# Attention scores and state-space products over 64 rows or over 128 rows with half of them zero

## The chip, the core and the metric

The kernel runs on one core of a Trainium2 chip. Five engines work beside each other, each through its own instructions in order: TensorE (PE, matrix products; PEld is its loading of the stationary operand), VectorE (DVE), ScalarE (ACT), GpSimd (POOL) and SyncE (SP, which issues the DMAs here). They meet through semaphores. The metric is the device time of one execution, in microseconds.

## The reference

One inference step of a two-layer decoder trunk. 512 prompt positions and 8 sample positions pass through the same weights. A layer is a half-step gated feed-forward block, a token mixer and a second feed-forward block, each followed by a layer norm. The mixer projects the input once and splits the columns among three branches and three gates:

```python
def _mixer(x, prev, n_prev_valid, lb, p):
    h = x @ p['w_in'] + p['b_in']
    q, k, v, mz, mxbc, mdt, hq, hf, hi, hg, gates = _split_cols(h)
    ya, nk, nv = _swa_attention(q, k, v, k_prev, v_prev, n_prev_valid, p['att_sinks'])
    ym, nconv, nssm = _mamba2(mz, mxbc, mdt, conv_prev, ssm_prev, ...)
    oh, nhg = _hgrn2(hq, hf, hi, lb, hg_prev)
    ...
    merged = g_att * (ya @ p['w_br_att']) + g_ssm * (ym @ p['w_br_ssm']) + g_hg * (yh @ p['w_br_hg'])
    return merged @ p['w_out'], ...
```

Two products matter here. In the attention there are 8 query heads of width 64 and 2 key heads (groups of 4 query heads share one), with a window of 128 positions:

```python
s = jnp.einsum('bnqkgd,bnskd->bnkgqs', qb, kb) * (HEAD_DIM ** -0.5)     # per key head k, over d = 64
```

In the state-space branch there are 2 groups with a state of width 64, and in each chunk of 128 positions

```python
w = jnp.einsum('bctgn,bcsgn->bctsg', Cc, Bc)[..., None] * decay * dt    # per group g, over n = 64
```

Both sum over 64 elements only, once for each of two groups.

## The kernel before

**Layout.** Activations lie transposed: channels on the 128 partitions, positions along the free dimension (520 columns, the first 512 the prompt's). A projection's 128 output channels are one tile. So one key tile `k` holds key head 0 on rows 0 to 63 and key head 1 on rows 64 to 127, and a query tile `q` of pair i holds head i on the upper rows and head 4+i on the lower. In the state-space branch the tiles `bm` (B) and `cm` (C) hold group 0 on rows 0 to 63 and group 1 on rows 64 to 127.

**The dense products.** Every weight multiplication (`gemm`, lines 166 to 179) splits both operands into a high and a low part and issues three matmuls of 128x128 by 260 columns for each 128 channels, lines 177, 178 and 179 (and 409 to 411 in the feed-forward blocks). Weights come in by DMA (tile `ws`), ACT casts the high part (`wh`, lines 73 and 90) and DVE subtracts it for the low part (`wl`, lines 74 and 91). The small products of the branches are plain f32 matmuls; the trace shows each of these as two MATMUL records, so "x2" below is one of them.

**The mixer.** `mixer` (line 557) emits first the HGRN2 branch (four heads, `hgrn_head`), woven with the input projections; then the four attention pairs, woven with the first merge (gates and output projection of the HGRN2 branch); then the state-space branch (`mamba`), and the two other merges. A scheduler then puts each engine's instructions in order from estimated times and priorities, so that in the built program the small products of a branch stand singly among the dense matmuls.

**Attention.** `attention_pair` (line 1102) takes, for each of four blocks of 128 queries, the scores of both groups: `q[rows]` is stationary, `k[rows]` moves, 128 or 256 columns wide, with `rows` the 64 rows of the group (line 1130). Each lands in a PSUM tile of the tag `s` (three of them). DVE adds the position bias and takes the maximum (line 1136); ACT takes the exponential (1148); DVE divides (1155); PE transposes (1165), the transposes are copied out (1167), and PE multiplies by the values (1175). A layer has 4 pairs x 4 blocks x 2 groups = 32 score matmuls.

**State-space branch.** `mamba` walks over four chunks c. Per chunk, line 939 takes the products of B and C for the two groups, again over 64 rows each; DVE masks them (942), builds the decay (945) and multiplies (947); PE multiplies by the values (954) and the state (960) and forms the new state (968). A layer has 8 matmuls of line 939. The sample positions are updated on DVE and POOL meanwhile (`mamba_sample`).

**Two tiles for the HGRN2 heads.** `self.att` (line 1342) is two tiles of 128x512, set to zero once by POOL at the start. `hgrn_head` writes the allowed places of its decayed products into them (lines 683 to 693, heads 0 and 2 into the first, 1 and 3 into the second) and PE reads them at line 735. The places never written stay zero.

Of the kernel before, what the change touches and what calls it, by code (L numbers as in the profile page):

```python
# [19 lines left out]
P = 128  # L20
NL = 2
NT = 520
TA = 260
TP = 512
# [101 lines left out]
class Kernel:  # L126
# [755 lines left out]
    def mamba(self, l):  # L882
        nc = self.nc
# [11 lines left out]
        bm, cm = xa[4], xa[5]  # L895
# [5 lines left out]
            nc.vector.tensor_copy(self.sp["z"][:, 8 * j : 8 * j + 8], z[j][:, TP:])  # L901

        self.mamba_sample(l, dt, dta)
        y = [self.slot(name="my", cols=TP) for _ in range(4)]
        state = None
        for c in range(4):
            cs = slice(c * P, (c + 1) * P)
            ab = []
            for g in (0, 1):
                a = self.slot(name="mab")  # L910
# [18 lines left out]
            if c:  # L929
                cw_t = self.slot(name="mcw")  # L930
                cw = cw_t[:, :TP].rearrange("p (h t) -> p h t", t=P)
                for g in (0, 1):
                    rows = slice(64 * g, 64 * g + 64)
                    nc.scalar.activation(cw[rows], ab[g][rows], AF.Exp)
                nc.vector.tensor_tensor(cw, cw, cm[:, cs].unsqueeze(1).to_broadcast([P, 4, P]), op=ALU.mult)
            pcb = [self.bank("s"), self.bank("s")]
            for g in (0, 1):
                rows = slice(64 * g, 64 * g + 64)
                nc.tensor.matmul(pcb[g][:, :P], lhsT=bm[rows, cs], rhs=cm[rows, cs], start=True, stop=True)
            for g in (0, 1):  # L940
                cbm = self.sm(P, "cbm")
                nc.vector.tensor_tensor(cbm, pcb[g][:, :P], self.tri, op=ALU.mult)
                for hh in range(4):
                    k = c * 8 + 4 * g + hh
# [4 lines left out]
                for jj in (0, 1):  # L949
                    for e in (0, 1):  # L950
                        hh, rows = 2 * jj + e, slice(64 * g, 64 * g + 64)
# [3 lines left out]
                for jj in (0, 1):  # L955
                    for e in (0, 1):
                        hh, rows = 2 * jj + e, slice(64 * g, 64 * g + 64)
# [9 lines left out]
            for g in (0, 1):  # L967
                nc.tensor.matmul(
                    pst[64 * g : 64 * g + 64, :256], lhsT=btok[:, 64 * g : 64 * g + 64], rhs=xw[:, 256 * g : 256 * g + 256],
                    start=True, stop=True,  # L970
# [7 lines left out]
                nc.vector.tensor_tensor(new, new, pst[:, :256], op=ALU.add)  # L978
            state = new
        nc.sync.dma_start(self.ap["o_pssm"][l], state)  # L980

        ssq = self.slot(name="mss", cols=TP)
        for j in range(4):
# [97 lines left out]
    def attention_lin(self, l, aq):  # L1081
# [13 lines left out]
        for i in range(4):  # L1095
# [3 lines left out]
            aq[i] = q  # L1099
            yield  # L1100

    def attention_pair(self, l, i, aq):
        nc = self.nc
        q, k = aq[i], aq["k"]
        if i == 0:
            vt, v = self.slot(name="avt"), aq["v"]
            p = self.bank("s")
            for n in range(4):
                ns = slice(n * P, (n + 1) * P)
                nc.tensor.transpose(p[:, ns], v[:, ns], self.ident)  # L1110
            nc.scalar.copy(vt[:, :TP], p)
            aq["vt"] = vt
        vt = aq["vt"]
        bias = self.slot(name="abias", cols=TP)
        nc.sync.dma_start(bias, self.ap["c_abias"][:, i * TP : (i + 1) * TP])
        sink = self.par[l][:, 161 + 8 * i : 169 + 8 * i]
        sc = [self.sample_slot() if i % 2 else self.slot(name="asc", cols=TP) for _ in range(4)]
        m, ng, den, es = (self.sm(8, x) for x in ("am", "ang", "aden", "aes"))

        def part(n, g):  # L1120
            w = 2 * P if n else P
            return sc[n][:, 2 * P * g : 2 * P * g + w], w

        yield
        for n in range(4):
            pp = [self.bank("s"), self.bank("s")]
            for g in (0, 1):
                s, w = part(n, g)
                rows = slice(64 * g, 64 * g + 64)
                nc.tensor.matmul(  # L1130
                    pp[g][:, :w], lhsT=q[rows, n * P : (n + 1) * P], rhs=k[rows, (n + 1) * P - w : (n + 1) * P], start=True, stop=True
                )
            for g in (0, 1):
                s, w = part(n, g)
                c = slice(2 * n + g, 2 * n + g + 1)
                nc.vector.tensor_tensor_reduce(
                    out=s, in0=pp[g][:, :w], in1=bias[:, 2 * P * (g + 1) - w : 2 * P * (g + 1)], scale=1.0, scalar=sink[:, c],
                    op0=ALU.add, op1=ALU.max, accum_out=m[:, c],
                )
        yield  # L1140
        nc.vector.tensor_scalar(ng, m, -1.0, None, op0=ALU.mult)
        nc.vector.tensor_tensor(es, sink, m, op=ALU.subtract)
        nc.scalar.activation(es, es, AF.Exp)
        for n in range(4):
            for g in (0, 1):
                s, w = part(n, g)
                c = slice(2 * n + g, 2 * n + g + 1)
                nc.scalar.activation(s, s, AF.Exp, bias=ng[:, c], accum_out=den[:, c])
        nc.vector.tensor_tensor(den, den, es, op=ALU.add)
        nc.vector.reciprocal(den, den)  # L1150
        for n in range(4):
            for g in (0, 1):
                s, w = part(n, g)
                c = slice(2 * n + g, 2 * n + g + 1)
                nc.vector.tensor_scalar(s, s, den[:, c], None, op0=ALU.mult)
        yield

        pt = {}
        for b in (0, 1):
            for g in (0, 1):  # L1160
                p = self.bank("s")
                lo = b * P
                for n in range(b, 4):
                    s, w = part(n, g)
                    nc.tensor.transpose(p[:, n * P : (n + 1) * P], s[:, w - P * (b + 1) : w - P * b], self.ident)
                pt[b, g] = self.slot(name="apt", cols=TP)
                (nc.scalar.copy if g else nc.vector.tensor_copy)(pt[b, g][:, lo:], p[:, lo:])
        yield
        pv = self.bank("s")
        for b in (0, 1):  # L1170
            for n in range(b, 4):
                ns = slice(n * P, (n + 1) * P)
                for g in (0, 1):
                    kb = (n - b) * P + 64 * g
                    nc.tensor.matmul(
                        pv[64 * g : 64 * g + 64, ns], lhsT=vt[:, kb : kb + 64], rhs=pt[b, g][:, ns],
                        start=b == 0 and n == 0, stop=b == 1 and n == 3,
                    )
        yh, yl = self.out_slot(F32R, "yah"), self.out_slot(F32R, "yal")
        nc.scalar.copy(yh[:, :TP], pv)  # L1180
        nc.vector.tensor_tensor(yl[:, :TP], pv, yh[:, :TP].bitcast(F32), op=ALU.subtract)
        self.at_out.append((yh, yl))
        yield
# [360 lines left out]
```

## Time and profile before

| what | value |
|---|---|
| median of 3 runs | 2606.45 us (2605.48 to 2608.71) |
| the profiled execution | 2604.06 us |
| its span, first to last instruction | 2602.3 us |
| busy: PE / DVE / ACT / POOL | 98% / 75% / 48% / 27% |
| mean granted TensorE clock | 0.992 |
| DMA queues' share of the 16 engines' time | 36.3% |

Busy time of PE overlaps itself, because a matmul's record runs on while the next one has started: the cadence is read from the distance between starts. The position in the span tells the stage: the first layer's attention lies at about 556 to 636 us, its state-space chunks at about 723 to 790 us; the second layer's lie about 1290 us later.

### The profile page before, as it was taken

What the parts mean: (1) busy time and instruction counts of PE and PEld (TensorE: products, weight loads), DVE (VectorE), ACT (ScalarE), POOL (GpSimd) and SP (SyncE); (2) the same over time, 40 slices, a digit from 0 to 9 for tenths busy, and PEclk for the clock granted to TensorE, in tenths of its full rate; (3) what the DMA queues carried; (4) which work ended last, traced back from release to release, by engine and by line L of the source; (5) the groups of instructions that cost most, each with busy time, mean ns of one, the idle gap of its engine ahead of it and who ended that gap; (6) DMA issues with size and microseconds to landing.
All of it is one profiled execution on the core that took longest, in us unless ns stands there. A gap on an engine that the chain in (4) does not pass through costs nothing.

```text
span 2602.3 us, 51878 instructions
## 1 busy us (share of the span) xinstructions
PE 2543.6 (98%) x20784; PEld 2474.7 (95%) x20784; DVE 1949.4 (75%) x3690; ACT 1250.4 (48%) x2358; POOL 694.6 (27%) x635
## 2 busy tenths in 40 slices
PE   8999999999999999999999999999999999999997
PEld 8999999898989999999989999999989899999997
DVE  8795988864685598868897858989546845978586
ACT  6352566443534473434663524764435344635255
POOL 1121243300143441212331212433001434413124
PEclk9999999999999999999999999999999999999999
DMA  6332356412242343232532414564123423333233
GB/s 208 105 122 82 127 178 217 149 68 83 99 141 91 122 138 106 90 114 82 186 128 93 141 55 150 171 219 145 57 84 112 139 90 122 138 98 107 89 125 119
DMA packets 134066, 318.17 MB, mean 122 GB/s; under 512 B 20452, under 2 KB 56516, under 8 KB 133824
## 3 DMA queue, kind: packets, MB, share of 16 engines
q1 hardware_dynamic: 133824, 314.86, 36.3%
q8 instruction: 163, 2.67, 0.4%
q14 instruction: 79, 0.65, 0.1%
HBM read 302.93 MB, written 11.88 MB: 121 GB/s over the span
## 4 chain that ended last, share of the span: by engine, by line
PE 73%; DVE 15%; DMA 4%; issue 3%; ACT 3%; POOL 3%; SPq 0%; POOLq 0%; ACTq 0%; DVEq 0%
PE g L177 15%; PE g L178 15%; PE g L179 15%; PE g L409 5%; PE g L411 5%; PE g L410 5%; DVE wl L91 3%; PE s L409 2%; PE s L411 2%; PE s L410 2%; DMA ws<-in_w_gu 1%; PE s L1130 1%; DVE y L249 1%; DMA smp<-r8d 1%; DVE xl L253 1%
## 5 line engine op out<-in xcount | busy, mean ns | idle before, releaser
L177 PE MATMUL g<-xh,wh 128*128 128x260 f32 (+1 forms) x2336 | 669.1, 287 | 7.5 <-ACT xh L1407 5.7
L178 PE MATMUL g<-xl,wh 128*128 128x260 f32 (+1 forms) x2336 | 668.7, 286 | 3.6 <-DVE xl L253 2.7
L179 PE MATMUL g<-xh,wl 128*128 128x260 f32 (+1 forms) x2336 | 668.2, 286 | 1.9 <-DVE wl L91 1.9
L90 ACT CAST wh<-ws 128x1024 fp32r<-128x1024 f32 (+1 forms) x382 | 389.9, 1024 | 376.6 <-PE g L178 252.4
L91 DVE TENSOR_TENSOR wl<-ws,wh 128x1024 fp32r<-128x1024 f32 (+1 forms) x382 | 469.4, 1231 | 117.4 <-ACT wh L90 116.6
L177 PEld LDWEIGHTS g<-xh,wh 128*128 128x128 f32 (+1 forms) x2336 | 439.5, 188 | 17.5 <-issue 6.1
L178 PEld LDWEIGHTS g<-xl,wh 128*128 128x128 f32 (+1 forms) x2336 | 439.2, 188 | 12.0 <-issue 4.2
L179 PEld LDWEIGHTS g<-xh,wl 128*128 128x128 f32 (+1 forms) x2336 | 439.6, 188 | 9.5 <-issue 4.1
L73 ACT CAST wh<-ws 128x1024 fp32r<-128x1024 f32 (+1 forms) x288 | 265.4, 942 | 295.9 <-PE g L178 161.7
L179 PE MATMUL g<-hh,wl 128*128 128x260 f32 x1408 | 396.1, 283 | 0.0
L178 PE MATMUL g<-hl,wh 128*128 128x260 f32 x1408 | 396.0, 283 | 0.0
L177 PE MATMUL g<-hh,wh 128*128 128x260 f32 x1408 | 391.8, 282 | 1.6 <-DVE y L275 1.6
L74 DVE TENSOR_TENSOR wl<-ws,wh 128x1024 fp32r<-128x1024 f32 (+1 forms) x288 | 320.3, 1118 | 87.1 <-ACT wh L73 86.0
L105 POOL TENSOR_TENSOR ws<-ws 128x512 f32<-128x512 f32 x72 | 136.2, 1892 | 632.0 <-DMA ws<-in_w_gu 260.0
L177 PEld LDWEIGHTS g<-hh,wh 128*128 128x128 f32 x1408 | 263.0, 188 | 2.1 <-DVE y L275 2.0
L178 PEld LDWEIGHTS g<-hl,wh 128*128 128x128 f32 x1408 | 264.7, 188 | 0.1
L179 PEld LDWEIGHTS g<-hh,wl 128*128 128x128 f32 x1408 | 264.6, 188 | 0.2
L409 PE MATMUL g<-xh,wh 128*128 128x260 f32 x864 | 246.3, 286 | 2.6 <-ACT wh L73 2.5
L410 PE MATMUL g<-xl,wh 128*128 128x260 f32 x864 | 245.0, 284 | 0.0
L411 PE MATMUL g<-xh,wl 128*128 128x260 f32 x864 | 242.4, 284 | 1.9 <-DVE wl L74 1.9
L409 PEld LDWEIGHTS g<-xh,wh 128*128 128x128 f32 x864 | 164.4, 190 | 4.8 <-ACT wh L73 3.7
L409 PE MATMUL g<-sx,wh 128*128 128x260 f32 x576 | 164.7, 286 | 4.3 <-ACT wh L73 4.3
(407 smaller groups left out, 5721.6 us busy)
## 6 DMA issues: line engine op xcount, KB each, us to landing
ws<-in_w_gu SPq DMA_DIRECT2D x208, 512.0 KB
ws<-in_w_in SPq DMA_DIRECT2D x132, 512.0 KB
ws<-in_w_dn SPq DMA_DIRECT2D x96, 512.0 KB
ws<-in_w_out SPq DMA_DIRECT2D x32, 512.0 KB
ws<-in_w_dn SPq DMA_DIRECT2D x32, 384.0 KB
smp<-r8d SPq DMA_DIRECT2D x48, 256.0 KB
ws<-in_w_br SPq DMA_DIRECT2D x24, 512.0 KB
smp<-in_hgr SPq DMA_DIRECT2D x16, 256.0 KB
```

The source lines that it names most:

```text
L73: nc.scalar.copy(h[:, :n], s[:, :n])
L74: nc.vector.tensor_tensor(lo[:, :n], s[:, :n], h[:, :n].bitcast(F32), op=ALU.subtract)
L90: nc.scalar.copy(h[:, :n], s[:, :n])
L91: nc.vector.tensor_tensor(lo[:, :n], s[:, :n], h[:, :n].bitcast(F32), op=ALU.subtract)
L105: nc.gpsimd.tensor_tensor(pa[:, b], u[:, a], u[:, b], op=ALU.add)
L177: nc.tensor.matmul(out, lhsT=h[:, wc], rhs=xh[:, c0:c1], start=st, stop=False)
L178: nc.tensor.matmul(out, lhsT=h[:, wc], rhs=xl[:, c0:c1], start=False, stop=False)
L179: nc.tensor.matmul(out, lhsT=lo[:, wc], rhs=xh[:, c0:c1], start=False, stop=en)
L249: nc.vector.scalar_tensor_tensor(y, y, gn, rb, op0=ALU.mult, op1=ALU.mult)
L409: nc.tensor.matmul(out, lhsT=h[:, wc], rhs=xh, start=first and k == 0, stop=False, **go)
L410: nc.tensor.matmul(out, lhsT=h[:, wc], rhs=xl, start=False, stop=False, **go)
L411: nc.tensor.matmul(out, lhsT=lo[:, wc], rhs=xh, start=False, stop=k == HK - 1, **go)
```

## The change

The products no longer pick 64 rows of both operands. The stationary operand is the whole tile of 128 rows, with both groups, and the moving operand is a tile in which the other group's 64 rows are zero. The result is the same sum. The two zero-padded tiles are made in the storage of the two `att` tiles: `by_group` zeroes the other group's half on POOL and copies the group's own half on ACT, once per layer for the keys (in the first attention pair) and once per layer for `cm`. In the first layer `restore_heads` sets both tiles back to zero after the state-space branch, because the HGRN2 heads of the second layer rely on it.

```diff
         self.mamba_sample(l, dt, dta)
+        self.by_group(cm)
...
             for g in (0, 1):
-                rows = slice(64 * g, 64 * g + 64)
-                nc.tensor.matmul(pcb[g][:, :P], lhsT=bm[rows, cs], rhs=cm[rows, cs], start=True, stop=True)
+                nc.tensor.matmul(pcb[g][:, :P], lhsT=bm[:, cs], rhs=self.grp[g][:, cs], start=True, stop=True)
...
         nc.sync.dma_start(self.ap["o_pssm"][l], state)
+        if l < NL - 1:
+            self.restore_heads()
...
+    def by_group(self, t):
+        nc = self.nc
+        self.grp = [a.rearrange("p c t -> p (c t)") for a in self.att]
+        for g in (0, 1):
+            rows, other = slice(64 * g, 64 * g + 64), slice(64 - 64 * g, 128 - 64 * g)
+            nc.gpsimd.memset(self.grp[g][other], 0.0)
+            nc.scalar.copy(self.grp[g][rows], t[rows, :TP])
+
+    def restore_heads(self):
+        for t in self.att:
+            self.nc.gpsimd.memset(t, 0.0)
...
             aq["vt"] = vt
+            self.by_group(k)
...
-                rows = slice(64 * g, 64 * g + 64)
                 nc.tensor.matmul(
-                    pp[g][:, :w], lhsT=q[rows, n * P : (n + 1) * P], rhs=k[rows, (n + 1) * P - w : (n + 1) * P], start=True, stop=True
+                    pp[g][:, :w], lhsT=q[:, n * P : (n + 1) * P], rhs=self.grp[g][:, (n + 1) * P - w : (n + 1) * P], start=True, stop=True
                 )
```

Line numbers behind the change are larger: the scores of line 1130 stand at 1146, the new memsets at 1111 and 1116, the new copies at 1112.

On PE the order of all matmuls stays as it was, in both layers; only the operands of the 80 products change. Here is a piece of the difference in the first attention pair of the first layer (`att_1042` is the first of the two tiles, `att_1044` the second, `aq` a query tile, `ak` the keys, `g` and `s` PSUM tiles):

```order
-L1130 MATMUL s<-ak,aq 128x256
-L179 MATMUL g<-xh,wl 128x260
-L1130 MATMUL s<-ak,aq 128x256
-L177 MATMUL g<-xh,wh 128x260
-L178 MATMUL g<-xl,wh 128x260
-L1130 MATMUL s<-ak,aq 128x128
+L1146 MATMUL s<-att_1042,aq 128x256
+L179 MATMUL g<-xh,wl 128x260
+L1146 MATMUL s<-att_1044,aq 128x256
+L177 MATMUL g<-xh,wh 128x260
+L178 MATMUL g<-xl,wh 128x260
+L1146 MATMUL s<-att_1042,aq 128x128
```

Nothing moved: each score keeps its neighbours and reads a zero-padded tile in place of half of the keys.

On POOL four memsets enter per layer, between the last sample products of the HGRN2 branch (lines 780 and 786) and the first convolution tile of the state-space branch (line 811). Before:

```order
L780 TENSOR_TENSOR smp<-smp 128x512
L786 TENSOR_TENSOR smp<-smp 128x512
L811 MEMSET cb 128x3
L814 COPY cb<-scv 128x8x3
L825 COPY pcv<-cb 128x3
```

and after:

```order
L780 TENSOR_TENSOR smp<-smp 128x512
L786 TENSOR_TENSOR smp<-smp 128x512
L1111 MEMSET att_1042 64x512
L1111 MEMSET att_1044 64x512
L1111 MEMSET att_1042 64x512
L1111 MEMSET att_1044 64x512
L811 MEMSET cb 128x3
L814 COPY cb<-scv 128x8x3
```

The first two belong to the keys and the other two to `cm`; the latter pair has to wait until the last scores of the layer have been read.

On ACT the copies of the keys stand far ahead of the first score, among the last two HGRN2 heads (`ho`, `yhh`, `hit` are tiles of these):

```order
 L683 COPY att_1044<-s 64x4x64
+L1112 COPY att_1042<-ak 64x512
 L743 ACTIVATE ho,hss<-s 128x128 x4
 L718 COPY hit<-s 128x512
@@ -394,68 +395,69 @@
 L517 ACTIVATE aq<-g,qb_1054 128x260
 L535 CAST yhh<-hy 128x512
+L1112 COPY att_1044<-ak 64x512
 L543 CAST yhh<-s_o 128x8
```

Each is placed behind the last work that the HGRN2 heads have for its tile on this engine. The two copies of `cm` stand together among the projections of the gate z, and the two memsets of `restore_heads` on POOL about the last chunk. DVE and SP keep their order.

## Rows read from the trace of the kernel before

**Rows 1.** The page, chain that ended last, by engine.
```profile
PE 73%; DVE 15%; DMA 4%; issue 3%; ACT 3%; POOL 3%; SPq 0%; POOLq 0%; ACTq 0%; DVEq 0%
```
**Rows 2.** Stretches: start:end, length, busy us by engine, clock, DMA share, GB/s.
```profile
556.00:600.00 44.00, 44.00 (x338) 38.08 (x338) 24.92 (x77) 20.57 (x53) 0.00 (x0) 1.00 0.22 73
...
723.00:760.00 37.00, 33.64 (x282) 30.18 (x280) 33.52 (x88) 12.12 (x23) 18.01 (x15) 1.00 0.53 169
760.00:790.00 30.00, 29.82 (x257) 26.30 (x258) 27.71 (x77) 11.68 (x21) 11.14 (x11) 1.00 0.28 98
...
2012.00:2049.00 37.00, 34.99 (x269) 30.95 (x269) 33.39 (x87) 11.07 (x21) 17.79 (x15) 0.91 0.56 170
```
**Rows 3.** One line's instructions: count, ns min/median/max, first and last start, forms.
```profile
L1130 PE MATMUL s<-ak,aq x128: 272/376/481, 557.1 to 1916.9; 64*128 64x256 f32 x96, 64*128 64x128 f32 x32
...
L939 PE MATMUL s<-mxa x32: 272/323/374, 723.7 to 2070.2; 64*128 64x128 f32 x32
```
**Rows 4.** Timeline of PE, attention: start, duration, line, operands.
```profile
572.32 0.49 PE L1130 MATMUL s<-ak,aq 64*128 64x128 f32 x2
572.74 0.39 PE L177 MATMUL g<-xh,wh 128*128 128x260 f32 x1
...
576.51 0.28 PE L179 MATMUL g<-xh,wl 128*128 128x260 f32 x1
576.63 0.28 PE L177 MATMUL g<-xh,wh 128*128 128x260 f32 x1
576.84 0.70 PE L1130 MATMUL s<-ak,aq 64*128 64x256 f32 x2
577.47 0.39 PE L178 MATMUL g<-xl,wh 128*128 128x260 f32 x1
577.69 0.28 PE L179 MATMUL g<-xh,wl 128*128 128x260 f32 x1
```
**Rows 5.** Timeline of PE, three scores in a row.
```profile
563.06 1.13 PE L1130 MATMUL s<-ak,aq 64*128 64x256 f32 x6
564.12 0.39 PE L177 MATMUL g<-yhh,wh 128*128 128x260 f32 x1
```
**Rows 6.** Timeline of PE, an f32 product over 128 rows, 260 columns.
```profile
1277.59 0.28 PE L178 MATMUL g<-hl,wh 128*128 128x260 f32 x1
1277.71 0.60 PE L229 MATMUL s<-ht,inv_d 128*128 128x260 f32 x2
1277.95 0.47 PE L179 MATMUL g<-hh,wl 128*128 128x260 f32 x1
1278.27 0.28 PE L177 MATMUL g<-hh,wh 128*128 128x260 f32 x1
```
**Rows 7.** Timeline of PE, an f32 product over 128 rows, 128 columns.
```profile
501.77 0.28 PE L179 MATMUL g<-xh,wl 128*128 128x260 f32 x1
501.89 0.38 PE L738 MATMUL s<-hst,hep 128*128 128x128 f32 x2
502.03 0.37 PE L177 MATMUL g<-xh,wh 128*128 128x260 f32 x1
502.24 0.28 PE L178 MATMUL g<-xl,wh 128*128 128x260 f32 x1
```
**Rows 8.** Timelines, a division on DVE and the transposes behind it.
```profile
578.25 1.40 DVE L1155 TENSOR_SCALAR asc<-asc,aden 128x256 f32<-128x256 f32 x5
...
584.24 1.03 PE L1165 MATMUL s<-ident,asc 128*128 128x128 f32 x8
```
**Rows 9.** POOL's memset of 128x512 as one line's instructions.
```profile
L1332 POOL MEMSET att<- x2: 524/524/524, 1.8 to 2.3; 128x512 f32 x2
```
**Rows 10.** Timelines of POOL, ACT and PE; in brackets idle time before, and releaser.
```profile
641.70 0.10 POOL L811 MEMSET cb<- 128x3 f32 x1 [124.65 <-PE s L1175]
...
557.19 0.58 ACT L1111 COPY avt<-s 128x512 f32<-128x512 f32 x1 [1.48 <-PE s L1110]
...
542.11 1.06 PE L735 MATMUL s<-hit,att 128*128 128x128 f32 x8
```

## The prediction

> **What bounds the kernel now.** I read the page first. In the chain that ended last, PE has 73% and DVE 15% [rows 1], so an edit pays where PE is on that chain and nothing else is late. Then the two stages that the change touches, by stretches. In the attention of the first layer PE is busy for all of 44.00 us, DVE for 24.92 and ACT for 20.57, POOL not at all [rows 2]: PE alone sets the pace there. In the state-space chunks it is otherwise: DVE has 33.52 of 37 us in 723 to 760 and 27.71 of 30 in 760 to 790 [rows 2]; PE waits in the first and both are nearly full in the second. Next the two lines themselves: 128 records of line 1130 and 32 of line 939 [rows 3], two records a product, so 64 scores (48 of 256 columns, 16 of 128) and 16 products of B and C (128 columns). Last the timeline of PE around single products, because PE's busy time overlaps itself: what a product costs is read from starts.
>
> **What one product over 64 rows costs.** Dense matmuls start 0.12 us apart (576.51 to 576.63) [rows 4]. A score of 256 columns starts 0.21 after its predecessor, the next dense matmul 0.63 after the score, the one behind that another 0.22 later [rows 4]. That is 1.06 us from predecessor to second successor, where 0.24 would do without it: 0.82 us. The 0.21 and the 0.22 are each 0.1 above cadence, so PE seems to empty itself before and behind it, and inside it the second record does not overlap the first as it might. With 128 columns the middle step is 0.42 (572.32 to 572.74) [rows 4], and with the same ends 0.85, less 0.24: 0.61 us.
>
> **What one over 128 rows costs.** The trace has f32 products over all rows, standing singly among the same dense matmuls. With 260 columns (line 229): 0.12, 0.24 and 0.32, together 0.68, less 0.24: 0.44 us [rows 6]. With 128 columns (line 738): 0.12, 0.14 and 0.21, together 0.47, less 0.24: 0.23 us [rows 7]. Twice the second is 0.46, so 256 columns cost 0.44 to 0.46; I take 0.44, the row of almost the same width. A single product thus saves 0.82 - 0.44 = 0.38 us at 256 columns and 0.61 - 0.23 = 0.38 at 128: the saving is the two ends and the pause inside, not the columns.
>
> **Scores.** In each layer's attention three scores of 256 columns stand in a row, and three take 1.06 us [rows 5] where one alone takes 0.63: the third adds 0.43 and the second nothing, so two of different groups run beside each other. With the ends (0.21 + 0.22 - 0.24) the three cost 1.25 us; as 128-row products 3 x 0.44 = 1.32. The change loses 0.07 there, twice. The other 58 scores stand singly (42 of 256 columns, 16 of 128; I counted them in the timelines of both layers), and the order on PE stays as it is. 58 x 0.38 = 22.0, less 0.1: 21.9 us. PE has no idle time in that stage into which this could vanish [rows 2].
>
> The Trainium skill speaks against the change at this place. In "TensorE: Matmul & The Clock Gate", Part 3 (packing small matmuls), products in different row groups run concurrently; and in its section "Why this matters for your kernels" a single product over 32 rows takes the time of one over 128. The trace agrees on the first where two such products are neighbours [rows 5]; on the second it differs, since a single one over 64 rows holds the dense stream 0.82 us against 0.44 [rows 4, 6]. By these two rules alone single products would gain nothing, and the sum would be 0.
>
> **What is late next in the attention.** The softmax of one pair runs while PE does the scores of the next. The divisions of pair 0 end on DVE at 578.25 + 1.40 = 579.65, and PE begins to transpose them at 584.24 [rows 8]: 4.6 us to spare. Between these PE does seven single scores of pair 1 (from 572.32 on) and comes 7 x 0.38 = 2.7 us earlier: 1.9 remain. So I charge nothing. DVE and ACT have 19 and 23 us free in 44 [rows 2] and keep up with a stretch that becomes some 6 us shorter.
>
> **Products of B and C.** Each of the 16 stands singly and saves 0.38 on PE, 6.1 us in all. What of it reaches the end lies between 0 and 6.1. Chunks 0 and 1 (four products a layer) lie in the stretch paced by DVE and by the loads that it waits for: nothing. Chunks 2 and 3 lie in 760 to 790, PE on the chain with DVE at 92% [rows 2]: I take half of 8 x 0.38, 1.5 us.
>
> **Memsets and copies.** Eight memsets of 64x512 and two of 128x512 on POOL, eight copies of 64x512 on ACT. A memset of 128x512 took 0.524 us, a copy of 512 columns 0.58 [rows 9, 10]; the half-height forms are not in the trace, so I bound them by 0 and by these. With the cover gone: 10 x 0.52 + 8 x 0.58 = 9.9 us; I take 0, because of the cover. Keys: POOL idles for 124.65 us up to 641.70 [rows 10], and the last read of the second tile by head 3 ends at 542.11 + 1.06 = 543.2 [rows 10], so memset and copy are through by about 545; the first score comes at 557.1 [rows 3]. The memsets for `cm` wait in POOL's queue for the last score; behind them stands line 811, which before the change began at 641.70 after PE's line 1175, later than the scores. The copies for `cm` fall on ACT, 48% busy over the span, among the projections of z, some 14 us before line 939. `restore_heads` holds POOL for 1.05 us in chunk 3 of one layer, where it has 11.14 of 30 us busy [rows 2].
>
> **Sum.** 21.9 + 1.5 = 23.4 us less. Against the profiled execution (2604.06, of which 2602.3 is span) that is 2580.7. This execution lies 2.4 us under the median of the runs shown; from the median, 2606.45 - 23.4 = 2583.0, and that is the forecast.
>
> **Clock.** In 2012 to 2049 the granted clock is 0.91 [rows 2]: 0.09 x 37 = 3.3 us lost, part of the stretch at 1.2 GHz after PE had waited for DVE. The same stage of the first layer has 1.00 [rows 2]. Such a stretch can come or go with shifted waits: 3.3 us either way.
>
> **Rivals.**
> 1. The gain comes back in the softmax. For it: DVE and ACT have in-order queues, and the 1.9 us above is small. Against: 43% of DVE's time is idle in that stage [rows 2]. If pair 1 and pair 3 gave all theirs back, half of 21.9 would be lost: 2606.45 - 11 - 1.5 = 2594.
> 2. A product over 64 rows costs what one over 128 rows costs in the same place, and the longer starts in rows 4 belong to f32 scores as such. Then nothing is gained: 2606. Against it: lines 229 and 738 are f32 too and have the short ends [rows 6, 7]. The second rule of the Trainium skill cited above would give this.
> 3. Slower. PE is held at the first product of each stage, because its padded tile is not ready: the first score (557.1) or line 939 (723.7) waits for POOL's memset or ACT's copy, and behind it on PE stand all dense matmuls. It decides from 11.7 us of waiting a layer (23.4 / 2); at 15 us the time is 2606.45 - 23.4 + 30 = 2613. For it: POOL's queue is in order. Against: the keys' tile would have to be ready 12 + 12 us later than worked out above.
>
> **How the numbers follow.** Forecast 0.83, rival 1 0.12, rival 2 0.03, rival 3 0.02. A measurement of this kernel tells about 0.2% (5 us) from no change. Forecast and rival 1 are faster: 0.95; rival 2 is the same: 0.03; rival 3 slower: 0.02. The range: downward, all of the 6.1 us of line 939 and 3.3 of clock, 2606.45 - 21.9 - 6.1 - 3.3 = 2575; upward it takes in rival 1 with 2594, to 2595 with the runs' own spread.
>
> **What the changed profile would show.** Right: a 256-column product of line 1146 has starts of 0.12, 0.24 and 0.32 around it and one of 128 columns 0.12, 0.14 and 0.21; the first layer's attention (first score to last transpose) is 11 us shorter, as is the second's; stretches 723 to 760 are no shorter; POOL's memsets end long before the first score. Wrong: starts of 0.2 before and behind the padded products (rival 2); idle time of PE before line 1165, released by DVE line 1155 (rival 1); idle time before the first line 1146, released by POOL or ACT (rival 3). A gain above 31 us or below 11 would refute the sum itself.

## The result, and the profile after

The changed kernel takes 2578.56 us (median of 4 runs, 2577.37 to 2583.22) beside 2606.34 for the kernel before: a ratio of 0.9895, interval 0.9878 to 0.9912, so 27.8 us or 1.05% less. Measured again beside other runs of the kernel before (experiment 4) the ratio was 0.9909 (0.9895 to 0.9922). The forecast was 2583.0, the range 2575 to 2595. The profiled execution has a span of 2576.1 us where the one before had 2602.3.

The page's chain by engine and its busy times, which answer to [rows 1]:

```profile
PE 2513.6 (98%) x20784; PEld 2471.3 (96%) x20784; DVE 1948.8 (76%) x3690; ACT 1255.2 (49%) x2366; POOL 694.1 (27%) x645
...
PE 73%; DVE 15%; DMA 4%; issue 3%; POOL 3%; ACT 2%; SPq 0%; POOLq 0%; ACTq 0%; DVEq 0%
```

The number of matmul records is what it was (20784), and the chain has the same shares but for one per cent of ACT. Nothing became the bound that was not. A change that shortens a stage which PE alone paces leaves no mark in the shares; it shows in the stretches. The view of stretches (start:end, length, busy us of PE, PEld, DVE, ACT and POOL, granted clock, DMA share, GB/s), at the places that answer to [rows 2]:

```profile
553.80:597.80 44.00, 44.00 (x379) 42.97 (x378) 27.25 (x85) 21.05 (x54) 0.00 (x0) 1.00 0.23 75
708.00:745.00 37.00, 33.34 (x267) 30.18 (x266) 33.43 (x87) 10.68 (x21) 17.24 (x15) 0.91 0.54 167
745.00:775.00 30.00, 30.00 (x274) 27.58 (x273) 28.32 (x77) 13.00 (x23) 12.50 (x13) 1.00 0.31 100
```

In the first 44 us of the attention PE now does 379 matmul records instead of 338, and its weight loads are busy for 42.97 us instead of 38.08: the dense stream is closed up. In 745 to 775 (before, 760 to 790) 274 records instead of 257 fit into the same 30 us. Only 708 to 745 has not gained, and there the clock is 0.91, which it was not before.

The scores as one line's instructions (count, ns minimum, median and maximum, first and last start), which answer to [rows 3]:

```profile
L1146 PE MATMUL s<-att,aq x128: 270/378/383, 554.9 to 1890.4; 128*128 128x256 f32 x96, 128*128 128x128 f32 x32
```

The median record is as long as before (378 ns against 376), only the longest fell from 481 to 383 ns: durations show little of the gain, starts show all of it. The timeline of PE around single scores, for [rows 4], in the first layer of the changed kernel (start, duration, line, operands):

```profile
567.69 0.28 PE L179 MATMUL g<-yhh,wl 128*128 128x260 f32 x1
567.82 0.38 PE L1146 MATMUL s<-att,aq 128*128 128x128 f32 x2
567.95 0.36 PE L177 MATMUL g<-xh,wh 128*128 128x260 f32 x1
568.16 0.28 PE L178 MATMUL g<-xl,wh 128*128 128x260 f32 x1
...
571.05 0.28 PE L177 MATMUL g<-xh,wh 128*128 128x260 f32 x1
571.17 0.59 PE L1146 MATMUL s<-att,aq 128*128 128x256 f32 x2
571.41 0.47 PE L178 MATMUL g<-xl,wh 128*128 128x260 f32 x1
571.72 0.28 PE L179 MATMUL g<-xh,wl 128*128 128x260 f32 x1
```

Read the starts. A score of 256 columns: 0.12, 0.24, 0.31, together 0.67 where two dense starts alone would be 0.24: it costs 0.43. One of 128 columns: 0.13, 0.13, 0.21, so 0.23. These are the steps of [rows 6, 7]: against [rows 4] the step in front fell from 0.21 to 0.12 and the one from the score to the next dense product from 0.63 to 0.24, while the last rose from 0.22 to 0.31.

How long the whole stages are now is read from two lines, the first transposes of the values and the first product of the attention's sample positions behind the four pairs. Before:

```profile
L1110 PE MATMUL s<-ident,av x8: 272/272/273, 556.6 to 1848.5; 128*128 128x128 f32 x8
...
L1219 PE MATMUL x<-skt,qm x32: 272/274/325, 643.6 to 1936.8; 128*64 128x130 f32 x32
```

and after:

```profile
L1126 PE MATMUL s<-ident,av x8: 272/272/273, 554.4 to 1832.8; 128*128 128x128 f32 x8
...
L1235 PE MATMUL x<-skt,qm x32: 272/274/325, 630.4 to 1910.1; 128*64 128x130 f32 x32
```

First starts give the first layer: 643.6 - 556.6 = 87.0 before, 630.4 - 554.4 = 76.0 after. Taken from the records themselves to the hundredth, the same distance was 87.03 and 86.99 us in the two layers before, 75.93 and 75.96 after. That is 11.10 + 11.03 = 22.1 us, where the scores were forecast at 21.9.

The second stage is that of the state-space chunks, from the first transpose of a chunk (line 918, or 919 where a line stands above it) to the first product of the norm behind them (line 552). All profiled executions side by side, attention in its two layers, then the chunks in theirs:

| kernel | attention | chunks, first layer | chunks, second layer |
|---|---|---|---|
| before | 87.03, 86.99 | 73.76 | 74.96 |
| before, profiled again (b1) | 87.03, 86.99 | 73.75 | 75.01 |
| changed | 75.93, 75.96 | 73.82 | 72.97 |
| changed, again (a4) | 75.93, 75.96 | 72.92 | 73.00 |
| scores alone (a1) | 75.93, 75.96 | 75.09 | 75.09 |
| products of B and C alone (a2) | 87.03, 86.99 | 74.75 | 73.10 |
| no padding (a3) | 75.97, 75.97 | 72.86 | 73.26 |

The attention repeats to 0.05 us from execution to execution. The chunks don't: two profiles of the changed kernel have 73.82 and 72.92 us in the first layer. Both have a stretch at half clock (1.2 GHz) there, and the kernel before has none there (below).

### The profile page after: what moved, and what is told of

Its sections match the earlier page's. It is cut to its first block, busy times and chain, and to the rows that moved or that the text cites. A ratio compares the mean times of both kernels' runs of the same rounds, so it can differ in the third digit from the quotient of the medians.

```text
span 2576.1 us, 51903 instructions
## 1 busy us (share of the span) xinstructions
PE 2513.6 (98%) x20784; PEld 2471.3 (96%) x20784; DVE 1948.8 (76%) x3690; ACT 1255.2 (49%) x2366; POOL 694.1 (27%) x645
## 4 chain that ended last, share of the span: by engine, by line
PE 73%; DVE 15%; DMA 4%; issue 3%; POOL 3%; ACT 2%; SPq 0%; POOLq 0%; ACTq 0%; DVEq 0%
PE g L178 15%; PE g L177 15%; PE g L179 15%; PE g L409 6%; PE g L411 5%; PE g L410 5%; DVE wl L91 3%; PE s L409 2%; PE s L411 2%; PE s L410 2%; DMA ws<-in_w_gu 1%; DVE y L249 1%; DMA smp<-r8d 1%; DVE xl L253 1%; DVE wl L74 1%
## 5 line engine op out<-in xcount | busy, mean ns | idle before, releaser
L177 PEld LDWEIGHTS g<-xh,wh 128*128 128x128 f32 (+1 forms) x2336 | 438.5, 188 | 10.2 <-ACT xh L1423 5.7
```

The costliest lines, as they stand in the source:

```text
L177: nc.tensor.matmul(out, lhsT=h[:, wc], rhs=xh[:, c0:c1], start=st, stop=False)
```

## The experiments

Two explanations stood beside each other for the gain itself: that the cost sits at the borders between products over 64 and over 128 rows (and in the pause inside a single one), or that an f32 product over 64 rows is dear as such. And it was open how much each half of the change gives, and whether the padding is free. The order of all matmuls on PE is the same in before, the changed kernel and a1 to a3.

**1. Scores alone (a1).** The changed kernel, with the products of B and C taken back:

```diff
-        self.by_group(cm)
...
-                nc.tensor.matmul(pcb[g][:, :P], lhsT=bm[:, cs], rhs=self.grp[g][:, cs], start=True, stop=True)
+                rows = slice(64 * g, 64 * g + 64)
+                nc.tensor.matmul(pcb[g][:, :P], lhsT=bm[rows, cs], rhs=cm[rows, cs], start=True, stop=True)
```

> The change in the attention alone (scores over 128 rows; the products of B and C stay over 64). Theory (each single product over 64 rows costs PE 0.38 us more, and PE sets the pace in the attention): 58 x 0.38 - 0.1 = 21.9 us less than before, about 2584.4; the state-space stage unchanged. Rival (the 4.4 us beyond the forecast belong to the attention, by waits that the shorter scores remove): 26 us or more less, under 2581. Rival (the products of B and C carry more than the 1.5 us charged): also 21.9 here, and the rest in the other half.

Measured: 2584.31 us (2581.65 to 2594.39) beside 2608.13; ratio 0.9917 (0.9902 to 0.9931), by which it is 21.6 us less with an interval of 18 to 26 (the two medians differ by 23.8). The two lines of the stage in this kernel:

```profile
L1126 PE MATMUL s<-ident,av x8: 272/273/273, 554.9 to 1838.3; 128*128 128x128 f32 x8
...
L1235 PE MATMUL x<-skt,qm x32: 272/274/325, 630.8 to 1915.8; 128*64 128x130 f32 x32
```

630.8 - 554.9 = 75.9: the attention is as short as with the whole change. The scores give nearly all of it.

**2. Products of B and C alone (a2).** The changed kernel, with the scores taken back:

```diff
-            self.by_group(k)
...
+                rows = slice(64 * g, 64 * g + 64)
-                    pp[g][:, :w], lhsT=q[:, ...], rhs=self.grp[g][:, ...], start=True, stop=True
+                    pp[g][:, :w], lhsT=q[rows, ...], rhs=k[rows, ...], start=True, stop=True
```

> The change in the state-space branch alone (products of B and C over 128 rows; scores stay over 64). Theory (half of the products lie where DVE sets the pace, PE catches up nothing there): 0 to 3 us less than before, 1.5 the middle, 2604.8; the four singles of chunks 2 and 3 come 0.38 us earlier each in the second layer's trace. Rival (all 16 count): 6.1 us less, 2600.2.

Measured: 2603.59 us (2599.09 to 2608.24, 11 runs), ratio 0.9983 (0.9973 to 0.9992): 4.4 us less, interval 2.1 to 7.0. The expected middle of 1.5 lies outside it, the 6.1 of the rival inside. The stage of the second layer took 73.10 us instead of 74.96, so 1.9 us of the 8 x 0.38 = 3.0 that PE saves there. That is more than the 0.75 us a layer that the prediction charged. The first layer's stage got no shorter in this profile (74.75 instead of 73.76): it has 10.2 us at half clock, where the kernel before has none. Added to a1 the ratio gives 21.6 + 4.4 = 26.0, the size of the whole change within the intervals. That the halves work on each other is not seen; intervals of some 4 us either way can't exclude it.

**3. No padding (a3).** The changed kernel without `by_group` and `restore_heads`; the products read the unpadded tiles, so it leaves out the separation of the two groups.

```diff
-        self.by_group(cm)
-                nc.tensor.matmul(pcb[g][:, :P], lhsT=bm[:, cs], rhs=self.grp[g][:, cs], start=True, stop=True)
+                nc.tensor.matmul(pcb[g][:, :P], lhsT=bm[:, cs], rhs=cm[:, cs], start=True, stop=True)
-            self.restore_heads()
-            self.by_group(k)
-                    pp[g][:, :w], lhsT=q[:, ...], rhs=self.grp[g][:, ...], start=True, stop=True
+                    pp[g][:, :w], lhsT=q[:, ...], rhs=k[:, ...], start=True, stop=True
```

> All 80 products over 128 rows, but the moving operand is the unpadded tile, so both groups' products are summed (the separation of the groups is left out); no memsets, no copies, no restoring. Theory (memsets and copies are fully covered): the same as the changed kernel within 1 us. Rival (they cost POOL, ACT or a wait on PE something): up to 9.9 us less than the changed kernel.

Measured: 2581.15 us, ratio 0.9897 (0.9882 to 0.9911), beside 0.9909 (0.9895 to 0.9922) for the changed kernel in the same comparison. The intervals overlap, and neither stage is clearly shorter (attention 75.97 against 75.93, chunks 72.86 and 73.26 against 72.92 and 73.00 in a4): the memsets and copies are hidden, as far as these comparisons resolve. The attention is also as short here with the keys read from their own tile, so it is the 128 rows that count and not the tile. Where they lie in the changed kernel is seen on POOL and ACT (in brackets idle time before, and who ended it):

```profile
541.16 0.52 POOL L1111 MEMSET att<- 64x512 f32 x1 [10.11 <-PE s L735]
611.66 0.52 POOL L1111 MEMSET att<- 64x512 f32 x1 [69.98 <-PE g L179]
612.82 0.52 POOL L1111 MEMSET att<- 64x512 f32 x1 [0.64 <-PE s L1146]
628.54 0.10 POOL L811 MEMSET cb<- 128x3 f32 x1 [15.21 <-PE s L1191]
```

```profile
541.39 0.62 ACT L1112 COPY att<-ak 64x512 f32<-64x512 f32 x1
```

The second of the keys' two tiles is ready at 541.39 + 0.62 = 542.0 (the first at 531.1), and the first score comes at 554.9: 13 us to spare. The copies of `cm` end at 694.8, and line 939 first starts at 708.3. The two memsets for `cm` do wait for the last scores in POOL's queue, but line 811 behind them then still waits 15.21 us for PE's line 1191.

**4. The changed kernel again (a4).** No edit; it ties the three above to the changed kernel on the same chip.

> The changed kernel once more, for a tighter ratio and a second trace. Theory (sum 23.4 us, the rest of the 27.8 measured is the clock's half-rate stretches and the start of the program, which differ between executions): 23 to 28 us less than before; in the trace the two attentions are 11.0 us shorter each again, while the start (2.0 us earlier by 27 us into the span in the first trace) and the places at 1.2 GHz differ. Rival (the rest is of the change): the same start and the same places again.

Measured: 2583.81 us (2581.32 to 2586.51), 24.3 us under the 2608.13 beside it, as expected. Its attention is as short as in the first profile (table). With a1 at 2584.31 and a3 at 2581.15 the three cannot be told apart by their times; the products of B and C (4 us) are at the limit of what such a comparison resolves, and stage durations decide there.

**5. The kernel before, again (b1).** No edit; it shows what changes from execution to execution without any change.

> The kernel before once more, for a second trace. Theory (start and clock are of the execution, not of the change): the first 27 us and the places at 1.2 GHz differ by a few us from the first trace of before. Rival (they are of the program): the same start, and half rate again near 657, 985, 1354, 1736, 2040 and 2275 us.

Measured: 2604.54 us, span 2602.8. Both stages repeat to 0.05 us (table). But by 27 us into the span it is 1.5 us earlier than the first profile of the same program, and at the end it is 0.5 us later. The changed kernel's profile is 2.0 us earlier at 27 us; a difference of that size between two profiles can belong to the execution alone. Of the six stretches at half clock that were named, four come again, each 3.1 us earlier in the span, as the program itself is there by 2 to 3; one comes at 515 instead of 658; the last comes again at 2276 but lasts 3.4 us instead of 6.8. So their places belong in the main to the program, which the rival had, and one of six to the execution.

**6. Every score twice, over 64 rows (b2) and over 128 rows (b3).** The same loop around the score product, in the kernel before and in the changed one:

```diff
-                nc.tensor.matmul(
+                for _ in (0, 1):
+                    nc.tensor.matmul(
```

If the dear part is the border, a second product right behind the first one costs the same in either form; if it is the product over 64 rows itself, the second costs 0.82 us there.

> The kernel before with each score product issued twice in a row (the second overwrites the first with the same values). Theory (the extra cost is that of the ends, at the border between 64-row and 128-row products): the second product costs only its own columns, as the third of the three in a row did: 48 x 0.43 + 16 x 0.22 = 24 us more than before, 2630. Rival (a product over 64 rows is slower by itself, wherever it stands): 48 x 0.82 + 16 x 0.61 = 49 us more, 2655.

> The changed kernel with each score product issued twice in a row. Theory (ends): the second costs 48 x 0.44 + 16 x 0.22 = 25 us, so it stands 25 us above the changed kernel, and the distance to the doubled kernel over 64 rows is again about 24 us. Rival (each product over 64 rows is slower by itself): the distance doubles to about 46 us.

Measured: b2 2638.09 us, ratio 1.0121 (1.0105 to 1.0138) to before; b3 2612.81, ratio 1.0019 (1.0009 to 1.0030). Between them lie 25.3 us, as between their undoubled forms (24 to 28). The timeline of PE in b2:

```profile
564.26 1.14 PE L1131 MATMUL s<-ak,aq 64*128 64x256 f32 x8
565.33 0.39 PE L177 MATMUL g<-yhh,wh 128*128 128x260 f32 x1
...
573.68 0.28 PE L178 MATMUL g<-xl,wh 128*128 128x260 f32 x1
573.89 1.13 PE L1131 MATMUL s<-ak,aq 64*128 64x256 f32 x4
574.95 0.39 PE L179 MATMUL g<-xh,wl 128*128 128x260 f32 x1
575.18 0.29 PE L177 MATMUL g<-yhh,wh 128*128 128x260 f32 x1
```

and in b3:

```profile
572.84 0.29 PE L178 MATMUL g<-xl,wh 128*128 128x260 f32 x1
572.96 1.03 PE L1147 MATMUL s<-att,aq 128*128 128x256 f32 x4
573.64 0.47 PE L179 MATMUL g<-xh,wl 128*128 128x260 f32 x1
573.95 0.28 PE L177 MATMUL g<-yhh,wh 128*128 128x260 f32 x1
```

Over 64 rows the middle step, from the first product's start to the next dense one, is 1.06 us for two (573.89 to 574.95), 0.63 for one [rows 4]: the second adds 0.43. Over 128 rows it is 0.68 against 0.24: the second adds 0.44. So a product over 64 rows that follows one of its own kind costs no more than one over 128, and the 0.38 us is paid once for each stay among the dense products, for two as for one: 0.21 + 1.06 + 0.23 = 1.50 us in b2 against 0.12 + 0.68 + 0.31 = 1.11 in b3, a difference of 0.39 with two products as with one. Of it 0.09 lies in front (0.21 against 0.12) and the rest between the product's first start and the second dense one behind it. The stages say the same: b2's attention took 97.26 and 97.22 us, 10.2 a layer more than before; b3's 87.09 and 87.07, 11.1 more than the changed kernel's; a second price of 0.82 and 0.61 us would have added 24.5 a layer to b2's.

The totals rose by more than the expected 24 and 25 us, though: by 31 in b2, and in b3 by 29 to 34, as the changed kernel is taken at 2583.81 or 2578.56. Two attention stages make only 20.5 and 22.3 of it. The scheduler gave these two programs another order elsewhere, stages outside the attention are up to 5 us longer, and there is more half clock; that rest was not followed up. It is about alike in both, so the reading rests on the timelines and the stages, and the distance between the totals agrees with it.

**7. Could 64-row pairs be kept together instead? (b4)** Two products of different groups that are neighbours run beside each other [rows 5]; a pair of 256 columns would cost what a single one does, 0.82 us, against 2 x 0.43 = 0.86 for two padded singles; at 128 columns 0.61 against 2 x 0.23 = 0.46. To get neighbours, the scores of the kernel before were issued late, by priority:

```diff
-                nc.tensor.matmul(
+                with self.tc.high_priority(offset=-6000):
+                    nc.tensor.matmul(
```

> The kernel before with the scores' priority lowered by 6000, so that most of them stand next to each other in the order of PE (runs of up to six, the groups alternating) behind the merge instead of singly within it. Theory (two row groups run beside each other when they are neighbours): in the trace a pair of 256 columns costs about 0.5 us where PE has its PSUM tiles free, less than two padded ones (0.88); as a whole the kernel is slower than before, by 10 to 60 us, because the softmax then lies behind the merge with nothing to cover it. Rival (they run one behind the other): 0.86 a pair.

Measured: 2620.11 us (one run) beside 2606.84, slower than all 13 runs of the kernel before (up to 2614.14). The timeline of PE:

```profile
627.87 0.92 PE L1131 MATMUL s<-ak,aq 64*128 64x256 f32 x6
629.15 1.10 PE L1131 MATMUL s<-ak,aq 64*128 64x128 f32 x4 [0.36 <-DVE am L1137]
630.96 2.90 PE L1131 MATMUL s<-ak,aq 64*128 64x256 f32 x10 [0.71 <-DVE am L1137]
635.77 2.64 PE L1166 MATMUL s<-ident,asc 128*128 128x128 f32 x11 [1.91 <-DVE asc L1156]
```

The scores now stand in runs, but behind the merge instead of within it: PE waits for DVE to empty the PSUM tiles (0.36, 0.71) and for the softmax (1.91). Record by record, the two products of the first pair at 627.87 start 0.01 us apart and the third product 0.54 after them, as in [rows 5]: neighbours of two groups run together, and about the 0.5 us that was expected for a pair holds there. What a pair costs among dense products cannot be read from it, because DVE sets the pace of the runs. It suggests, without showing it, why the scores stood singly: they are issued one at a time, as a PSUM tile comes free. Pairs kept together inside the merge were not tried; by the prices above they would gain 0.04 us a pair at 256 columns and lose 0.15 at 128.

## Why the prediction was right, point by point

**The price of a product.** Right, and it carried the result. Forecast 0.82 and 0.61 us for one over 64 rows, 0.44 and 0.23 over 128; the changed kernel has 0.43 and 0.23 in the very places. The three in a row are dearer, as said: line 1146 of 559.69 has its successor at 560.79, 1.10 us instead of 1.06, and with their ends the three cost 1.30 us instead of 1.25 (1.32 forecast):

```profile
559.69 1.46 PE L1146 MATMUL s<-att,aq 128*128 128x256 f32 x6
560.79 0.47 PE L177 MATMUL g<-yhh,wh 128*128 128x260 f32 x1
```

The first rule cited, row groups run concurrently ("TensorE: Matmul & The Clock Gate", Part 3, of the Trainium skill), agrees with b2: four products of two groups in a row take 1.07 us (564.26 to 565.33), two of one group 1.06. The second, that a single product over 32 rows takes the time of one over 128 ("Why this matters for your kernels", on the same page of the Trainium skill), holds for 64 rows in b2 for the product itself, 0.43 against 0.44, but not for what it costs a dense stream. What it leaves out stands on another page of the Trainium skill, "TensorEngine Tiling (Array Packing)", Key Properties: changing the tiling mode drains the engine. A price for each stay that does not grow with the products in it agrees with that: 0.38 us in the runs here. That page of the Trainium skill gives no figure. The prediction had it as 0.1 us at each end and a pause inside. The single records of the score at 576.84 and of the one at 571.17 in the changed kernel show where it lies: 0.09 more in front (0.21 against 0.12), 0.10 more between the product's two records (0.32 against 0.22), and 0.20 more from the second record to the second dense product behind it (0.53 against 0.33).

What the prediction did not look at, and the trace shows, are the weight loads. PEld before:

```profile
576.51 0.19 PEld L177 LDWEIGHTS g<-xh,wh 128*128 128x128 f32 x1
576.84 0.29 PEld L1130 LDWEIGHTS s<-ak,aq 64*128 64x128 f32 x2
577.47 0.19 PEld L178 LDWEIGHTS g<-xl,wh 128*128 128x128 f32 x1 [0.33 <-issue]
```

and after:

```profile
571.05 0.31 PEld L1146 LDWEIGHTS s<-att,aq 128*128 128x128 f32 x2
571.38 0.19 PEld L178 LDWEIGHTS g<-xl,wh 128*128 128x128 f32 x1
```

In the dense stream a load starts 0.12 us ahead of its product, while the product in front still runs (576.51 for 576.63). At both borders of a 64-row score it doesn't: the score's load starts with the score (576.84), and the load of the next dense product with that product (577.47), after PEld has idled 0.33 us. With padding the score's load is again 0.12 ahead (571.05 for 571.17), and the next one 0.03. So it is in all 48 single scores whose neighbours are products of lines 177 to 179: a lead of 0.002 us at both borders before, of 0.12 and 0.03 after. Why a load does not run ahead across a border is not shown by any run.

**Scores, 21.9 us.** Right: 22.1 by the two stages, 21.6 (18 to 26) by a1's times.

**The softmax is late next, but not late enough (rival 1).** Right to a tenth. DVE and PE in the changed kernel, for [rows 8]:

```profile
573.83 1.40 DVE L1171 TENSOR_SCALAR asc<-asc,aden 128x256 f32<-128x256 f32 x5
...
577.09 1.03 PE L1181 MATMUL s<-ident,asc 128*128 128x128 f32 x8
```

The divisions end at 575.23 and the transposes begin at 577.09: the 1.9 us that were worked out. The view of waits lists none of PE from 553 to 632, before or after the change.

**Rivals 2 and 3.** Both refuted: the starts are 0.12 and 0.24 (rival 2), and the padded tiles of the keys and of `cm` are ready 13 us early (rival 3).

**Memsets and copies, nothing.** Right (a3). The half-height memset took 0.52 us, the copy 0.62.

**Products of B and C, 1.5 us.** This term of the sum was mis-sized. The step was: "Chunks 2 and 3 lie in 760 to 790, PE on the chain with DVE at 92% [rows 2]: I take half of 8 x 0.38, 1.5 us". In the second layer the stage lost 2.0 us (74.96 and 75.01 to 72.97 and 73.00). Lined up instruction by instruction, chunks 2 and 3 gave all of their 4 x 0.38 = 1.5 us, and chunks 0 and 1 kept 0.45 of theirs instead of none. The waits of PE (line, whom it waited for; us, times, longest) in 706 to 800 would have told it. Before:

```profile
PE s L954 <- DVE mab L947: 2.0, 1, 2.0
PE s L918 <- DVE my L963: 1.4, 1, 1.4
```

after, in 700 to 790:

```profile
PE s L954 <- DVE mab L947: 3.3, 1, 3.3
PE s L939 <- DVE mxd L923: 0.3, 1, 0.3
```

In chunks 0 and 1 the wait for DVE's line 947 grows from 2.0 to 3.3 and takes back most of the gain, as forecast. In chunks 2 and 3 PE waited for DVE once, 1.4 us in the first layer, in spite of DVE's 92%: an engine that is nearly full but hardly waited for leaves the pace to the other. In the first layer this gain is 1.3 to 2.2 us, read against a1 (75.09), since the first stage of before had no half clock; a2's profile, with 10.2 us of half clock there instead of a1's 6.8, shows only 0.3 (74.75). So by the two profiles of the changed kernel the term is 3.2 to 4.2 us, in line with a2's 4.4 by times (2.1 to 7.0).

**Clock, 3.3 us either way.** As a bound it held; what a stretch cost was less. One came in the first layer's chunks, whose clock of 1.00 the prediction had pointed at. The view of stretches for the kernel before in its second profile, the changed kernel and a1, in this order:

```profile
720.00:760.00 40.00, 36.47 (x302) 32.70 (x301) 36.44 (x96) 13.74 (x26) 20.32 (x17) 1.00 0.53 169
```

```profile
736.00:743.00 7.00, 7.00 (x43) 5.26 (x40) 7.00 (x15) 0.48 (x1) 3.92 (x3) 0.52 0.45 138
```

```profile
736.00:743.00 7.00, 7.00 (x43) 5.25 (x44) 7.00 (x15) 0.48 (x1) 3.92 (x3) 0.53 0.39 125
```

Both profiles of before have 1.00 through the first layer's chunks; all eight profiles of other kernels have 7 to 10 us at the lower level of 1.2 GHz there. It costs some 1.3 us: 75.09 in a1, whose stage is otherwise unchanged, against 73.76. That is net: the wait of 1.4 us at line 918 of before is absent in a1 and in the changed kernel, so part of the lost clock fell into time that PE waited before. It hides the gain of the products of B and C in the first layer, which is why that stage looks unchanged (73.82). What PE did before it, on the timelines of before, the changed kernel and a1:

```profile
749.91 0.66 PE L954 MATMUL s<-mab,mxd 128*64 128x128 f32 x8 [2.04 <-DVE mab L947]
```

```profile
735.00 0.66 PE L954 MATMUL s<-mab,mxd 128*64 128x128 f32 x8 [3.34 <-DVE mab L947]
```

```profile
735.25 0.66 PE L954 MATMUL s<-mab,mxd 128*64 128x128 f32 x8 [2.14 <-DVE mab L947]
```

In these two PE comes sooner to the same wait for DVE, and the clock falls 1.0 and 0.6 us after the wait has ended. But a1's wait is only 0.1 longer than that of before, and in the second layer of before a wait of 2.0 is followed by such a stretch too:

```profile
2039.03 0.66 PE L954 MATMUL s<-mab,mxd 128*64 128x128 f32 x8 [2.01 <-DVE mab L947]
```

So the wait's length doesn't decide it alone. Why the stretch comes with a change of scores only, which end some 80 us earlier, stays open.

**The sum.** 22.1 + 3.2 to 4.2 - 1.3 = 24.0 to 25.0 us by stages, forecast 23.4; by medians 27.8 in the first comparison and 24.3 in the second, whose intervals (23 to 32 and 20 to 27) hold it. That the sum came out so close is in part luck: the products of B and C were put some 2 us too low, and the half clock that came took 1.3 back. The two profiles differ by 26.2 in span: 24.1 in the four stages and 2.1 in the time up to the first attention. The stretches between the stages and behind them are up to 2.6 us shorter or longer and cancel; what makes these was not followed up.

## What to carry to other kernels

A product over part of the rows that stands alone in a stream of full-height products pays for its place, not for its size: here 0.38 us each, 58 times in 64, and its weights and those of the product behind it are not loaded ahead. Zero-padding the moving operand to full height is then worth it, if the zeros can be written under cover; where products of different row groups are neighbours it gains next to nothing (three in a row lost 0.05 us), for there the second is free already. What a stage gives is decided by who waits in it, not by who is nearly full: read the waits before halving a gain.

## What was not expected of the hardware

- A memset of 64x512 on POOL took 0.52 us, as long as one of 128x512 [rows 9]: half the rows saved nothing.
- A stretch at 1.2 GHz can change its place between two executions of one program: the kernel before had 3.4 us of it at 658 us into the span in one profile, and none there but 3.4 at 515 in the other. Most did not: five of six came again at about their place.
- A weight load that runs 0.12 us ahead of its product in a dense stream of 128-row products had no lead (0.002 us) into and out of a 64-row product.
